# Expert outputs stored in 8 KB runs from half partitions, and three semaphores by turns for the Pool queue

## The chip, the cores and the metric

The kernel runs on one core of a Trainium2 chip. The metric is the device time of one execution in microseconds (us). Four runs before the change took 180.51 to 180.61 us, with a median of 180.54.

TensorE (PE) multiplies matrices, VectorE (DVE) and ScalarE (ACT) copy and apply functions, GpSimd (POOL) and SyncE (SP) issue transfers. Sixteen DMA engines carry out the transfers. A transfer is cut into packets, one for each contiguous run of bytes, and these are spread over the sixteen engines. Each issuing engine has its own queue, in which transfers start in the order in which they were issued.

## The reference

Eight experts, each with its own 256 tokens and two weight matrices; everything is float32 in memory:

```python
n_experts, capacity, hidden, expert_hidden = 8, 256, 512, 2048
# x [8, 256, 512], w1 [8, 512, 2048], w2 [8, 2048, 512]
h = np.matmul(x, w1)
h = np.maximum(h, 0)
return np.matmul(h, w2).astype(np.float32)
```

The weights are 64 MB, x and the output 4 MB each.

## The kernel before

**Transfers in.** x comes in two parts: SP loads a quarter as float32 (`x_head`, line 131), which VectorE casts to bfloat16 (line 132); Pool loads the rest and casts it on the way (line 146). All weights are loaded by Pool and cast to bfloat16 on the way (line 184), in the order of the list `loads` (lines 114 to 120): w1 and w2 of experts 0 and 1, then of 2 and 3, w1 of 4 and 5, w2 of 4, w2 of 5, w1 and w2 of 6, w1 of 7, and w2 of 7 in two halves. There are four places (`NS`) for the weights of an expert, so from expert 4 on a load waits until the expert four before it has used its weights (lines 166 to 170). w2 of experts 2 and 3 also waits for the transposes, since x lies in its place.

Every load adds 16 to a semaphore when it has landed. There is one such semaphore for each kind of weight and place, and one for the second half (`d_w`, `d_half`, lines 85 to 90). `landed[i]` is the semaphore and the count of load i. SP waits for the loads one after the other and passes each on to TensorE (lines 136 to 138).

**Computation.** TensorE transposes x (lines 290 to 318). VectorE and ScalarE copy the results from PSUM to `xT`, each one half of the tokens, four times (`copy_xt`, lines 193 to 197). In PSUM the columns stand by residue of the token number, and the copy puts them into the order that makes token `p * 2 + m` of an expert row `p` of output tile `m`.

Then the loop over experts (`expert`, line 397) has two halves of the hidden layer, 64 matmuls into `h_ps` with four ReLU activations on ScalarE, and 32 matmuls into `o_ps[0]` and `o_ps[1]`, one PSUM bank for 128 tokens each. VectorE copies each `o_ps[m]` to `out_sb[:, e, m, :]` (line 211); the last one is ScalarE's (line 231). TensorE takes `c_o` at the end of each half of the hidden layer (line 386), so that it doesn't write over outputs that are still to be copied.

**Transfers out.** Partition `p` of `out_sb` has tokens `2p` and `2p + 1` of each expert, 4 KB that are contiguous in the output. Experts 0 to 6 go out in one transfer by Pool, here called the gather (line 187), expert 7 in one by SP (line 140). Pool issues the gather when a small store of 1 KB (line 175) has landed. This store stands in the queue ahead of the second half of w2 of expert 7 and so tells when the loads before it are done. VectorE adds to `s_event` after experts 4 and 6 (line 214); the small store waits for the first of these, the gather for the second.

Of the kernel before, what the change touches and what calls it, by code (L numbers as in the profile page):

```python
# [8 lines left out]
FP32 = mybir.dt.float32  # L9
# [7 lines left out]
def kernel(  # L17
# [8 lines left out]
    P = 128  # L26
    E, C, H = x.shape
    F = w1.shape[2]
    MC = C // P
# [3 lines left out]
    R = E * C // P  # L33

    HEAD = 4

    NS = 4
# [8 lines left out]

    x_v = x.rearrange("e (pp r) k -> (e pp) (r k)", r=R)
    w1_v = w1.rearrange("e (p ko) n -> p e (ko n)", ko=K1)  # L50
    w2_v = w2.rearrange("e (p h j) n -> p e h (j n)", h=2, j=JH)
    out_v = out.rearrange("e (p mo) k -> p e (mo k)", mo=MC)


    places, free = {}, FIRST_FREE
# [1 line left out]
    def allot(name, shape, dtype):  # L57
        nonlocal free
        places[name] = free
        t = nc.alloc_sbuf_tensor_at(name, shape, dtype, offset=free)  # L60
        free += math.prod(shape[1:]) * mybir.dt.size(dtype)
        return t


    out_sb = allot("out_sb", [P, E, MC, H], FP32)
    w1_sb = allot("w1_sb", [P, NS, K1 * F], BF16)
    w2_sb = allot("w2_sb", [P, NS, K2 * H], BF16)
    xT = allot("xT", [P, K1, MC, E * P], BF16)
# [4 lines left out]
    x_sb = w2_sb[:, 2, :]  # L73
    X_AT = W2_AT + 2 * K2 * H * 2

    xt_ps = [nc.alloc_psum_tensor(f"xt_ps{i}", [P, R // MC, P], BF16) for i in range(MC)]
    h_ps = [nc.alloc_psum_tensor(f"h_ps{i}", [P, GJ * C], FP32) for i in range(UG)]
    o_ps = [nc.alloc_psum_tensor(f"o_ps{i}", [P, H], FP32) for i in range(MC)]

    def sem(name):  # L80
        return tc.alloc_semaphore(name)

    d_w = {
        (w, i): sem(f"d_w{w}_{i}")
        for w, slots in [(1, (0, 2, 3)), (2, (0, 1, 2, 3))]
        for i in slots
    }
    d_half, d_pool, d_last = sem("d_half"), sem("d_pool"), sem("d_last")  # L90


    s_event = sem("s_event")
    s_pe, v_last = sem("s_pe"), sem("v_last")

    def after_transposes(n):
        return s_pe, n

    def after_hidden(e, groups):
        return s_pe, K1 * MC + e * (NG + MC) + groups  # L100

    def after_outputs(e, halves):
        return s_pe, K1 * MC + e * (NG + MC) + NG + halves
# [10 lines left out]
    loads = []  # L114
# [3 lines left out]
    for e in range(6, E - 1):  # L118
        loads += [(1, (e,), 0, 2), (2, (e,), 0, 2)]
    loads += [(1, (E - 1,), 0, 2), (2, (E - 1,), 0, 1), (2, (E - 1,), 1, 1)]  # L120
    landed, counts = [], {}
    for w, es, h, _ in loads:
        s = d_half if h else d_w[w, es[0] % NS]
        counts[id(s)] = counts.get(id(s), 0) + 16
        landed.append((s, counts[id(s)]))

# [6 lines left out]
    with tc.tile_critical(no_gpsimd_drain=True):  # L133

        sp = nc.sync
        for i, (w, es, h, n) in enumerate(loads):
            sp.wait_ge(*landed[i])
            sp.sem_inc((c_w1, c_w2)[w - 1], n * len(es) if w == 2 else len(es))
        sp.wait_ge(v_last, MC)
        sp.dma_start(  # L140
            out_v[:, E - 1, :], out_sb[:, E - 1].rearrange("p m h -> p (m h)")
        ).then_inc(d_last, 16)


        pool = nc.gpsimd
        pool.dma_start(x_sb[:, HEAD * H:], x_v[:, HEAD * H:]).then_inc(d_pool, 16)  # L146
        pool.memset(identity[:], 0.0).then_inc(s_event)  # L147
        pool.wait_ge(s_event, 1)

# [1 line left out]
            out=identity[:],  # L151
# [7 lines left out]
        for i, (w, es, h, n) in enumerate(loads):  # L159


            old = es[-1] - NS
            if w == 2 and 2 in es:
                tc.wait_critical_data_deps()
                pool.wait_ge(*after_transposes(K1 * MC))
            if old >= 0 and h == 0:
                if w == 1:
                    pool.wait_ge(*after_hidden(old, NG))
                else:
                    pool.wait_ge(*after_outputs(old, MC))  # L170
            if i == len(loads) - 1:


                pool.wait_ge(s_event, 3)
                pool.dma_start(  # L175
                    out_v[:16, 0, :16], out_sb[:16, 0, 0, :16]
                ).then_inc(d_pool, 16)
            e, ne, at_slot = es[0], len(es), es[0] % NS
            if w == 2:
                src = w2_v[:, e:e + ne, h:h + n, :].rearrange("p e h n -> p e (h n)")  # L180
                dst = w2_sb[:, at_slot:at_slot + ne, h * JH * H:(h + n) * JH * H]
            else:
                src, dst = w1_v[:, e:e + ne, :], w1_sb[:, at_slot:at_slot + ne, :]
            pool.dma_start(dst, src).then_inc(landed[i][0], 16)  # L184
        pool.wait_ge(s_event, 4)
        pool.wait_ge(d_pool, 32)
        pool.dma_start(  # L187
            out_v[:, :E - 1, :], out_sb[:, :E - 1].rearrange("p e m h -> p e (m h)")
        ).then_inc(d_pool, 16)

        def copy_xt(copy, ko, m):
            return copy(  # L194
                xT[:, ko, m].rearrange("k (ep r2) -> k ep r2", r2=R // MC),
                xt_ps[m][:].rearrange("k r2 ep -> k ep r2"),
            )


        dve = nc.vector  # L200
        dve.sem_inc(c_xt[0], 1)
        for ko in range(K1):
            dve.wait_ge(*after_transposes(ko * MC + 1))
            copy_xt(dve.tensor_copy, ko, 0).then_inc(c_xt[0])
        dve.sem_inc(c_o, MC)
        for e in range(E):
            for m in range(MC):
                if e == E - 1 and m == 1:
                    break
                dve.wait_ge(*after_outputs(e, m + 1))  # L210
                cp = dve.tensor_copy(out_sb[:, e, m, :], o_ps[m][:])  # L211
                cp.then_inc(v_last if e == E - 1 else c_o)
            if e in (4, E - 2):
                dve.drain().then_inc(s_event)  # L214
# [16 lines left out]
        act.copy(out_sb[:, E - 1, 1, :], o_ps[1][:]).then_inc(v_last)  # L231

# [3 lines left out]
        pe = nc.tensor  # L236
# [45 lines left out]
        def last_column(step):  # L282

            return (P - 1) * step * 2
# [25 lines left out]
                t.then_inc(s_pe)  # L310

        pe.wait_ge(s_event, 2)
        pe.wait_ge(d_pool, 16)
# [119 lines left out]


        pool.drain()
        pool.wait_ge(d_pool, 48).then_inc(s_event)
        pool.wait_ge(d_last, 16).then_inc(s_event)


# [28 lines left out]
```

## Time and profile before

| what | value |
|---|---|
| median of four runs | 180.54 us |
| the profiled execution, its own time | 180.51 us |
| its span, first to last instruction | 178.7 us |
| TensorE busy | 126.9 us, 71% of the span |
| ScalarE, VectorE, Pool busy | 38.7, 15.8 and 10.2 us |
| bytes read from and written to memory | 71.30 MB and 4.20 MB |
| Pool's queue, share of the 16 DMA engines' span | 97.3% |
| SP's queue | 2.4% |
| gather of experts 0 to 6 (3,584 KB), issue to landing | 12.9 us |
| store of expert 7 (512 KB), issue to landing | 4.7 us |
| x by SP (1,024 KB) and by Pool (1,536 KB after the cast) | 4.7 and 11.5 us |
| copy of one output tile, VectorE, 128 x 512 | 686 ns |
| copy of one part of xT, 128 x 1024: VectorE, ScalarE | 1,224 and 1,012 ns |

A packet's bytes are counted as written, so a load that casts float32 to bfloat16 reads twice as many as are shown. Windows are stretches of the span with the busy time of each engine, the DMA share (mean busy share of the 16 DMA engines; it can pass 1 a little, since a packet is counted where it starts) and the bytes moved in GB/s. "Us to landing" runs from the start of the issuing instruction until the semaphore has its full count, and so has the time in the queue in it. Beside these views the trace has a record of every DMA packet (start, duration, bytes, queue) and of every semaphore update at a landing.

### The profile page before, as it was taken

The page shows a single profiled execution, that of the slowest core. Times are in us where ns is not written, and L with a number is a line of the kernel's source. Part 1 is how long each engine was busy: PE and PEld are TensorE (multiplying, and loading weights), DVE is VectorE, ACT ScalarE, POOL GpSimd, SP SyncE. Part 2 cuts the span into 40 slices and gives each one's busy share as a digit, 9 for nine tenths or more (in the row PEclk, how much of TensorE's full clock was granted, in tenths as well). Part 3 has the DMA queues.
Part 4 walks back from the last instruction along what each step waited for, and adds up shares of the span by engine and source line. Part 5 has one row for each costly group of instructions (what it writes and reads, how often), then busy time and mean ns, then how long its engine had stood idle before and what let it go on. Part 6 is the DMA issues. An engine that isn't in the chain of part 4 may idle for free. (4 is left out here: it accounts for less than half of the span.)

```text
span 178.7 us, 2096 instructions
## 1 busy us (share of the span) xinstructions
PE 126.9 (71%) x832; PEld 89.4 (50%) x832; DVE 15.8 (9%) x20; ACT 38.7 (22%) x38; POOL 10.2 (6%) x21
## 2 busy tenths in 40 slices
PE   0008610793049999991079999999999999969950
PEld 0006600693014794791024884794695596369420
DVE  0204320000000200200000200200200200110010
ACT  0202420044000152062000251152063044015210
POOL 6100010000000002101000101100020000002000
PEclk9999999999559999999558999999999999999998
DMA  6999998998998999999899899999999989989996
GB/s 211 244 216 209 235 224 187 235 231 187 227 235 191 220 235 209 202 235 227 183 235 235 183 227 235 194 216 235 213 198 235 227 183 235 235 180 220 328 423 258
DMA packets 3744, 40.37 MB, mean 226 GB/s; under 512 B 288, under 2 KB 288, under 8 KB 1312
## 3 DMA queue, kind: packets, MB, share of 16 engines
q0 software_dynamic: 3456, 38.80, 97.3%
q1 hardware_dynamic: 288, 1.57, 2.4%
HBM read 71.30 MB, written 4.20 MB: 422 GB/s over the span
## 5 line engine op out<-in xcount | busy, mean ns | idle before, releaser
L264 PE MATMUL o_ps<-w_sb,hT 128*128 x256 | 60.3, 396 | 18.8 <-PEq L239 18.8
L264 PE MATMUL h_ps<-xT,w_sb 128*128 x512 | 60.6, 280 | 11.2 <-PEq L239 11.2
L264 PEld LDWEIGHTS h_ps<-xT,w_sb 128*128 x512 | 57.6, 146 | 15.1 <-issue 11.9
L225 ACT ACTIVATE hT<-h_ps 128x1024 bf16<-128x1024 f32 x32 | 32.7, 1023 | 109.6 <-PE h_ps L264 109.6
L264 PEld LDWEIGHTS o_ps<-w_sb,hT 128*128 128x128 bf16 x256 | 25.3, 101 | 51.2 <-issue 24.4
L211 DVE COPY out_sb<-o_ps 128x512 f32<-128x512 f32 x15 | 9.7, 686 | 139.7 <-PE o_ps L264 139.7
L264 PE MATMUL xt_ps<-identity,w_sb 128*128 128x128 bf16 x64 | 7.6, 312 | 15.5 <-PEq L239 15.5
L264 PEld LDWEIGHTS xt_ps<-identity,w_sb 128*128 x64 | 6.5, 147 | 16.3 <-issue 16.3
L184 POOL DMA_DIRECT2D w_sb<-in_w_dram x12 | 7.4, 618 | 105.2 <-PE h_ps L264 56.5
L194 ACT COPY xT<-xt_ps 128x1024 bf16<-128x1024 bf16 x4 | 4.0, 1012 | 11.8 <-PE xt_ps L264 11.8
L194 DVE COPY xT<-xt_ps 128x1024 bf16<-128x1024 bf16 x4 | 4.9, 1224 | 11.8 <-PE xt_ps L264 11.8
L187 POOL DMA_DIRECT2D out_dram<-out_sb x1 | 1.0, 962 | 33.1 <-DMA out_dram<-out_sb 33.1
L194 ACT ACT_TABLE_LOAD x1 | 1.3, 1283 | 7.0 <-DVE w_sb L132 7.0
L231 ACT COPY out_sb<-o_ps 128x512 f32<-128x512 f32 x1 | 0.6, 585 | 5.9 <-PE o_ps L264 5.9
L132 DVE CAST w_sb<-x_head 128x2048 bf16<-128x2048 f32 x1 | 1.2, 1227 | 5.5 <-DMA x_head<-in_x_dram 5.5
L175 POOL DMA_DIRECT2D out_dram<-out_sb x1 | 0.5, 509 | 14.7 <-DVEq L214 14.7
L146 POOL DMA_DIRECT2D w_sb<-in_x_dram x1 | 0.7, 679 | 0.8 <-POOLq L452 0.8
L150 POOL TENSOR_SCALAR_AFFINE_SELECT identity<-identity 128x128 bf16<-128x128 bf16 x1 | 0.3, 282 | 0.2 <-POOL identity L147 0.2
L147 POOL MEMSET identity<- 128x128 bf16 x1 | 0.2, 223 | 0.0
L452 POOL MEMSET const-float32-0.0<- 128x1 f32 x1 | 0.1, 92 | 0.2 <-issue 0.2
L452 POOL MEMSET const-bfloat16-1.0<- 128x1 bf16 x1 | 0.1, 95 | 0.0
L452 POOL MEMSET const-uint8-127<- 128x1 uint8 x1 | 0.1, 95 | 0.0
(1 smaller groups left out, 0.1 us busy)
## 6 DMA issues: line engine op xcount, KB each, us to landing
w_sb<-in_w_dram POOLq DMA_DIRECT2D x5, 4096.0 KB, 47.9
w_sb<-in_w_dram POOLq DMA_DIRECT2D x5, 2048.0 KB, 51.0
out_dram<-out_sb POOLq DMA_DIRECT2D x1, 3584.0 KB, 12.9
w_sb<-in_w_dram POOLq DMA_DIRECT2D x2, 1024.0 KB, 43.2
w_sb<-in_x_dram POOLq DMA_DIRECT2D x1, 1536.0 KB, 11.5
x_head<-in_x_dram SPq DMA_DIRECT2D x1, 1024.0 KB, 4.7
out_dram<-out_sb SPq DMA_DIRECT2D x1, 512.0 KB, 4.7
out_dram<-out_sb POOLq DMA_DIRECT2D x1, 1.0 KB, 33.6
```

What stands on the lines that cost most here:

```text
L132: nc.vector.tensor_copy(x_sb[:, :HEAD * H], x_head[:])
L146: pool.dma_start(x_sb[:, HEAD * H:], x_v[:, HEAD * H:]).then_inc(d_pool, 16)
L150: pool.affine_select(out=identity[:], in_=identity[:], compare_op=mybir.AluOpType.not_equal, fill=1.0, base=0, pattern=[[-1, P]], channel_ ...
L175: pool.dma_start(out_v[:16, 0, :16], out_sb[:16, 0, 0, :16]).then_inc(d_pool, 16)
L184: pool.dma_start(dst, src).then_inc(landed[i][0], 16)
L187: pool.dma_start(out_v[:, :E - 1, :], out_sb[:, :E - 1].rearrange("p e m h -> p e (m h)")).then_inc(d_pool, 16)
L194: return copy(xT[:, ko, m].rearrange("k (ep r2) -> k ep r2", r2=R // MC), xt_ps[m][:].rearrange("k r2 ep -> k ep r2"),)
L211: cp = dve.tensor_copy(out_sb[:, e, m, :], o_ps[m][:])
L225: act.activation(hT[:, g * GJ:(g + 1) * GJ, :].rearrange("p a c -> p (a c)"), h_ps[g % UG][:], mybir.ActivationFunctionType.Relu,).then_in ...
L231: act.copy(out_sb[:, E - 1, 1, :], o_ps[1][:]).then_inc(v_last)
L264: return pe.add_instruction(inst)
L452: nc = _bacc.Bacc("TRN2", target_bir_lowering=False, num_devices=1)
```

## The change

It has two parts.

1. *Semaphores.* The nine semaphores for Pool's transfers in and out (`d_w`, `d_half`, `d_pool`) become three, used by turns; `d_last` for SP's store stays. A transfer with number i uses semaphore i mod 3, and before it is issued Pool waits until transfer i - 3 has landed. The numbers are: 0 the part of x, 1 to 11 the loads but the last, 12 the small store, 13 the last load, 14 the gather, 15 a further store.

2. *Outputs.* Experts 0 to 5 are kept in pairs: the even one of a pair on partitions 0 to 63, the odd one on 64 to 127. A partition has four tokens of its expert, `4q` to `4q + 3`, which are 8 KB and contiguous in the output. Since a PSUM tile still has 128 tokens on 128 partitions, VectorE copies it in two halves of 64 partitions. For token `4q + 2t + m` to come out on row `t * 64 + q` of tile `m`, the columns of `xT` for these experts get another order, and each copy to `xT` becomes three (two for experts 0 to 5, one for 6 and 7). The gather has experts 0 to 5. Expert 6 goes out in a transfer of its own right behind it on Pool's queue, in runs of 4 KB as before, and expert 7 by SP as before. VectorE adds to `s_event` after experts 0, 5 and 6 instead of 4 and 6; the small store waits for the first, the gather for the second, expert 6's store for the third.

```diff
+    HP = P // 2
+    PAIRS = E // 2 - 1
+    out_pairs = out[:2 * PAIRS].rearrange("(i s) (q r) k -> s q i (r k)", s=2, r=2 * MC)
+    out_v = out.rearrange("e (p m) k -> p e (m k)", m=MC)
...
-    out_sb = allot("out_sb", [P, E, MC, H], FP32)
+    out_sb = allot("out_sb", [P, PAIRS, 2 * MC, H], FP32)
+    last_sb = allot("last_sb", [P, 2, MC, H], FP32)
...
-    d_half, d_pool, d_last = sem("d_half"), sem("d_pool"), sem("d_last")
+    d_pool, d_last = [sem(f"d_pool{i}") for i in range(3)], sem("d_last")
...
+    of_load = [i + 1 for i in range(len(loads) - 1)] + [len(loads) + 1]
+    small, bulk, bulk2 = len(loads), len(loads) + 2, len(loads) + 3
+
+    def landed(i):
+        return d_pool[i % 3], 16 * (i // 3 + 1)
...
+        def queue(i, dst, src):
+            if i >= 3:
+                pool.wait_ge(*landed(i - 3))
+            pool.dma_start(dst, src).then_inc(d_pool[i % 3], 16)
...
-            pool.dma_start(dst, src).then_inc(landed[i][0], 16)
+            queue(of_load[i], dst, src)
+        pool.wait_ge(*landed(small))
         pool.wait_ge(s_event, 4)
-        pool.wait_ge(d_pool, 32)
-        pool.dma_start(
-            out_v[:, :E - 1, :], out_sb[:, :E - 1].rearrange("p e m h -> p e (m h)")
-        ).then_inc(d_pool, 16)
+        queue(bulk, out_pairs, out_sb[:].rearrange("p i r h -> p i (r h)"))
+        pool.wait_ge(s_event, 5)
+        queue(bulk2, out_v[:, E - 2, :], last_sb[:, 0].rearrange("p m h -> p (m h)"))
...
         def copy_xt(copy, ko, m):
+            EP = 2 * PAIRS
+            for t in range(2):
+                copy(
+                    xT[:, ko, m, :EP * P].rearrange(
+                        "k (e t pp r4) -> k t e pp r4", e=EP, t=2, r4=R // 4
+                    )[:, t],
+                    xt_ps[m][:, :, :EP * (P // E)].rearrange(
+                        "k (r4 t) (e pp) -> k t e pp r4", t=2, e=EP
+                    )[:, t],
+                )
             return copy(
-                xT[:, ko, m].rearrange("k (ep r2) -> k ep r2", r2=R // MC),
-                xt_ps[m][:].rearrange("k r2 ep -> k ep r2"),
+                xT[:, ko, m, EP * P:].rearrange("k (ep r2) -> k ep r2", r2=R // MC),
+                xt_ps[m][:, :, EP * (P // E):].rearrange("k r2 ep -> k ep r2"),
             )
+
+        def copy_out(copy, e, m):
+            if e >= 2 * PAIRS:
+                return copy(last_sb[:, e - 2 * PAIRS, m, :], o_ps[m][:])
+            i, s = divmod(e, 2)
+            for t in range(2):
+                inst = copy(
+                    out_sb[s * HP:(s + 1) * HP, i, t * MC + m, :],
+                    o_ps[m][t * HP:(t + 1) * HP, :],
+                )
+            return inst
...
-            if e in (4, E - 2):
+            if e in (0, E - 3, E - 2):
                 dve.drain().then_inc(s_event)
...
-        pool.wait_ge(d_pool, 48).then_inc(s_event)
+        for i in (bulk, bulk2):
+            pool.wait_ge(*landed(i)).then_inc(s_event)
         pool.wait_ge(d_last, 16).then_inc(s_event)
```

More of the change, by code (lines that the diff above doesn't have):

```diff
@@ L51 @@
     w2_v = w2.rearrange("e (p h j) n -> p e h (j n)", h=2, j=JH)
-    out_v = out.rearrange("e (p mo) k -> p e (mo k)", mo=MC)
+    HP = P // 2
+    PAIRS = E // 2 - 1
+    out_pairs = out[:2 * PAIRS].rearrange("(i s) (q r) k -> s q i (r k)", s=2, r=2 * MC)
+    out_v = out.rearrange("e (p m) k -> p e (m k)", m=MC)
     places, free = {}, FIRST_FREE
@@ L81, in sem @@
         return tc.alloc_semaphore(name)
[L85 to L89, printed above, removed]
-    d_half, d_pool, d_last = sem("d_half"), sem("d_pool"), sem("d_last")
+    d_pool, d_last = [sem(f"d_pool{i}") for i in range(3)], sem("d_last")
     s_event = sem("s_event")
@@ L120 @@
     loads += [(1, (E - 1,), 0, 2), (2, (E - 1,), 0, 1), (2, (E - 1,), 1, 1)]
[L121 to L125, printed above, removed]
+    of_load = [i + 1 for i in range(len(loads) - 1)] + [len(loads) + 1]
+    small, bulk, bulk2 = len(loads), len(loads) + 2, len(loads) + 3
+    def landed(i):
+        return d_pool[i % 3], 16 * (i // 3 + 1)
     x_pool = ctx.enter_context(tc.tile_pool(name="x_pool", bufs=1))
@@ L136 @@
         for i, (w, es, h, n) in enumerate(loads):
-            sp.wait_ge(*landed[i])
+            sp.wait_ge(*landed(of_load[i]))
             sp.sem_inc((c_w1, c_w2)[w - 1], n * len(es) if w == 2 else len(es))
@@ L140 @@
         sp.dma_start(
-            out_v[:, E - 1, :], out_sb[:, E - 1].rearrange("p m h -> p (m h)")
+            out_v[:, E - 1, :], last_sb[:, 1].rearrange("p m h -> p (m h)")
         ).then_inc(d_last, 16)
         pool = nc.gpsimd
-        pool.dma_start(x_sb[:, HEAD * H:], x_v[:, HEAD * H:]).then_inc(d_pool, 16)
+        def queue(i, dst, src):
+            if i >= 3:
+                pool.wait_ge(*landed(i - 3))
+            pool.dma_start(dst, src).then_inc(d_pool[i % 3], 16)
+        queue(0, x_sb[:, HEAD * H:], x_v[:, HEAD * H:])
         pool.memset(identity[:], 0.0).then_inc(s_event)
@@ L174 @@
                 pool.wait_ge(s_event, 3)
-                pool.dma_start(
-                    out_v[:16, 0, :16], out_sb[:16, 0, 0, :16]
-                ).then_inc(d_pool, 16)
+                queue(small, out_pairs[0, :16, 0, :16], out_sb[:16, 0, 0, :16])
             e, ne, at_slot = es[0], len(es), es[0] % NS
@@ L183 @@
                 src, dst = w1_v[:, e:e + ne, :], w1_sb[:, at_slot:at_slot + ne, :]
-            pool.dma_start(dst, src).then_inc(landed[i][0], 16)
+            queue(of_load[i], dst, src)
+        pool.wait_ge(*landed(small))
         pool.wait_ge(s_event, 4)
-        pool.wait_ge(d_pool, 32)
-        pool.dma_start(
-            out_v[:, :E - 1, :], out_sb[:, :E - 1].rearrange("p e m h -> p e (m h)")
-        ).then_inc(d_pool, 16)
+        queue(bulk, out_pairs, out_sb[:].rearrange("p i r h -> p i (r h)"))
+        pool.wait_ge(s_event, 5)
+        queue(bulk2, out_v[:, E - 2, :], last_sb[:, 0].rearrange("p m h -> p (m h)"))
         def copy_xt(copy, ko, m):
+            EP = 2 * PAIRS
[8 more added lines that the diff above has]
+                )
             return copy(
-                xT[:, ko, m].rearrange("k (ep r2) -> k ep r2", r2=R // MC),
-                xt_ps[m][:].rearrange("k r2 ep -> k ep r2"),
-            )
+                xT[:, ko, m, EP * P:].rearrange("k (ep r2) -> k ep r2", r2=R // MC),
+                xt_ps[m][:, :, EP * (P // E):].rearrange("k r2 ep -> k ep r2"),
+            )
+        def copy_out(copy, e, m):
[8 more added lines that the diff above has]
+            return inst
         dve = nc.vector
@@ L210 @@
                 dve.wait_ge(*after_outputs(e, m + 1))
-                cp = dve.tensor_copy(out_sb[:, e, m, :], o_ps[m][:])
+                cp = copy_out(dve.tensor_copy, e, m)
                 cp.then_inc(v_last if e == E - 1 else c_o)
-            if e in (4, E - 2):
+            if e in (0, E - 3, E - 2):
                 dve.drain().then_inc(s_event)
@@ L230 @@
         act.wait_ge(*after_outputs(E - 1, MC))
-        act.copy(out_sb[:, E - 1, 1, :], o_ps[1][:]).then_inc(v_last)
+        copy_out(act.copy, E - 1, 1).then_inc(v_last)
         pe = nc.tensor
@@ L312 @@
         pe.wait_ge(s_event, 2)
-        pe.wait_ge(d_pool, 16)
+        pe.wait_ge(*landed(0))
         x_first = X_AT + last_column(K1)
```

## The prediction

> **What bounds the kernel now.** I read the page's slices first: the row of DMA shares shows whether the transfer engines ever rest.
>
> ```profile
> DMA  6999998998998999999899899999999989989996
> GB/s 211 244 216 209 235 224 187 235 231 187 227 235 191 220 235 209 202 235 227 183 235 235 183 227 235 194 216 235 213 198 235 227 183 235 235 180 220 328 423 258
> q0 software_dynamic: 3456, 38.80, 97.3%
> ```
>
> They rest only at both ends. A slice is 4.47 us and a packet of weights takes over 1 us, so the GB/s row beats; longer windows are steadier. Columns: busy times by engine, then PE clock, DMA share, GB/s written.
>
> ```profile
> 24.00:30.00 6.00, 0.00 (x0) 0.00 (x0) 0.00 (x0) 0.10 (x1) 0.07 (x1) 1.00 1.02 218
> 48.00:54.00 6.00, 2.40 (x6) 0.87 (x7) 0.00 (x0) 0.00 (x0) 0.00 (x0) 0.50 1.03 218
> 84.00:90.00 6.00, 0.00 (x0) 0.00 (x0) 0.00 (x0) 0.00 (x0) 0.00 (x0) 0.59 1.03 218
> 108.00:114.00 6.00, 6.00 (x31) 2.85 (x30) 0.27 (x1) 0.01 (x1) 0.00 (x0) 1.00 1.01 216
> 166.00:167.00 1.00, 1.00 (x6) 0.42 (x5) 0.00 (x0) 0.46 (x1) 0.00 (x0) 1.00 0.82 176
> 167.00:168.00 1.00, 1.00 (x6) 0.49 (x5) 0.00 (x0) 0.00 (x0) 0.00 (x0) 1.00 0.96 385
> 171.00:172.00 1.00, 1.00 (x7) 0.39 (x4) 0.00 (x0) 0.00 (x0) 0.00 (x0) 1.00 1.02 422
> 176.00:177.00 1.00, 0.00 (x0) 0.00 (x0) 0.00 (x0) 0.00 (x0) 0.00 (x0) 1.00 0.98 401
> 177.00:178.00 1.00, 0.00 (x0) 0.00 (x0) 0.00 (x0) 0.00 (x0) 0.00 (x0) 0.62 0.07 25
> ```
>
> Loads are cast, so 218 GB/s written is 436 GB/s read. A boundary between two loads lies inside 48 to 54 us (TensorE waits for w2 of experts 0 and 1 until 51.6) and doesn't show. At 167 us the stores take over at 422 GB/s and run to 177.3. In 84 to 90 TensorE is idle while the transfers run.
>
> The chain of waits names TensorE, but only up to the issue of the last store:
>
> ```profile
> 158.04 0.04 issue
> 158.09 7.32 PE h_ps L264 x64
> 165.40 6.97 PE o_ps L264 x32
> 172.37 0.02 issue
> 172.39 0.58 ACT out_sb L231
> ```
>
> Who decides after that? The last store is issued at 173.00, and the trace's packet records have its first packet on a DMA engine at 175.60, just as that engine ends the gather (all move in step, the last 0.47 us behind the first). At the start the same queue's x load, issued at 0.74, had a packet moving at 1.75. So the store could have run from 174.0 and stood 1.6 us behind the gather. The DMA engines are the bound from 1.75 to 177.3; a change matters if it opens a hole there, changes what a packet costs, or changes the ends.
>
> **The issue order.** The timeline of the Pool queue shows when each of the last transfers is issued:
>
> ```profile
> 107.25 0.53 POOL L184 DMA_DIRECT2D w_sb<-in_w_dram  x1 [6.59 <-PE h_ps L264]
> 114.20 0.53 POOL L184 DMA_DIRECT2D w_sb<-in_w_dram  x1 [6.43 <-PE o_ps L264]
> 129.43 0.51 POOL L175 DMA_DIRECT2D out_dram<-out_sb  x1 [14.69 <-DVEq L214]
> 129.93 0.55 POOL L184 DMA_DIRECT2D w_sb<-in_w_dram  x1
> 163.58 0.96 POOL L187 DMA_DIRECT2D out_dram<-out_sb  x1 [33.09 <-DMA out_dram<-out_sb]
> ```
>
> All weights are queued by 130.5, the last of them over 30 us before it moves. The trace's landing records (us): x 12.7; w1 of experts 0 and 1 at 32.1, w2 51.4; w1 of 2 and 3 at 70.8, w2 90.1; w1 of 4 and 5 at 109.5, w2 of 4 at 119.2, of 5 at 128.9; expert 6 138.5 and 148.2; w1 of 7 at 157.9, first half of its w2 162.8, the small store 163.0, second half 167.7, gather 176.5, last store 177.7.
>
> **Part 1, three semaphores by turns.** Transfer i is now issued only when i-3 has landed. Taking the wake as 0.59 us (the small store's landing at 162.99 to the gather's issue at 163.58), the loads go out at about 13.3 (w1 of 2 and 3), 32.7, 67.4 (still the wait for expert 1's hidden layer), then 71.4, 90.7, 110.1, 119.8, 129.5, 139.1, small store 148.8, second half of w2 158.5. Each time the queue still holds i-2 and i-1. In the middle that is at least two 2,048 KB loads, 19.4 us. It is least for the second half of w2: only the first half and the small store lie ahead, which the first DMA engine finishes at 162.03. The gather bounds the time from issue to first packet: 163.58 to 166.89, so at most 3.31 us. 157.91 + 0.59 + 3.31 = 161.8 is still 0.2 us before 162.03; the x load behind the SP load gives a like bound, 1.23 to 4.61. I take **0**; lower bound 0, upper bound below as a rival. Behind the waiting instruction on Pool stand only later transfers, each slowed as counted. The gather's own trigger, the small store, is in its old place in the queue, so the gather is issued at 163.6 as before, behind 4 us of load. SP's counts go by the same landings.
>
> **Part 2, the gather.** Before: 7 x 128 packets of 4 KB, 56 for each DMA engine. After: 3 x 128 of 8 KB and 128 of 4 KB, so 24 and 8. The packet records give the period on one DMA engine: 155.3 ns for 4 KB in the gather (65,536 B in 155.3 ns is the 422 GB/s above), 306.0 ns for 8 KB in the SP queue's uncast x load between 3.7 and 4.3 us. That is another direction of transfer, but it is the nearest row: 24 x (310.6 - 306.0) = **-0.11 us**. Bounds: 0, if 8 KB costs just two packets of 4 KB; -0.24, if the store reaches the loads' 436 GB/s (27.25 per DMA engine, 8 KB in 300.6 ns: 24 x 10.0). A loss is excluded as far as rows go: every steady row with larger packets is as fast or faster. One more transfer means one more completion packet per DMA engine: 6 ns from such a packet to the next in the store stage, **+0.01**; at most 0.06, which is 1% of a 6 us window with a boundary in it.
>
> The Trainium skill, "DMA: Bandwidth & Descriptors", section on the anatomy of a DMA from GpSimd, puts a fixed cost of about 2.0 us on each such transfer. By that the split into two stores would add 2.0 and give 182.4. The window 48 to 54 speaks against it in a full queue.
>
> The same page (why a DMA increments its semaphore by 16) says that a transfer is spread over the engines by its outermost dimension, and the new view of the output has an outermost dimension of 2. If that were kept, 2 of 16 engines would carry the gather. The two outer steps can join into one of 128 equal steps (64 rows of 8 KB are one expert's 512 KB, and the next expert begins there), so I expect 16; no row here shows a gather of that form.
>
> **Part 3, the copies.** Twelve output copies become 24 of half the partitions. From the groups: 686 ns each; if a half costs as much (bounds 343 and 686), an expert's copies take 2.7 us instead of 1.3. They hide under the next expert's hidden layer (7.28 us), whose two takes come 3.6 and 7.3 us on. The xT copies become three pieces each: the fixed part of a DVE copy is about 0.15 us (1,224 ns for 1,024 columns, 686 for 512), ScalarE's 0.16, so 2 x 0.15 x 4 rounds = 1.2 us more, at most 9.8 if each piece cost a whole copy. The transposes end at 24.1 and TensorE stands until 32.25 for w1: 8.1 us of cover. Even past it TensorE waits 9.7 us more for w2 at 51.6, and x lands long before. Were that cover gone, the first expert would start 1.2 us late; the stream of transfers, which sets the end, would not. The two plain experts' copies don't change, so the last store is still issued at 173.0, with 1.5 us to spare. **0**.
>
> **Part 4, the end.** After 177.7 come the closing barriers and one instruction that clears 26 semaphores in 179 ns; six fewer, at the 5 ns between two clears, **-0.03** (bounds 0 and -0.04).
>
> **Sum:** -0.11 + 0.01 - 0.03 = -0.13 us on the profiled execution (180.51, span 178.7 and 1.8 around it), which stands 0.03 under the median; taken off the median: 180.54 - 0.13 = **180.41**. Its own range is 180.26 (-0.24, -0.04, 0) to 180.60 (0, 0, +0.06).
>
> **Rivals.** (a) *The 8 KB runs bring nothing*: 180.52. For it: 4 KB packets already leave only 3% between 422 and 436. (b) *The store reaches the load's rate*: 180.26; for it the 436, against it the measured 306 ns. (c) *A late second half*, on the slow side: the second half of w2 reaches the queue after 162.03, all engines stop, and everything behind moves by the gap, since stores follow loads. It decides when landing-to-first-packet passes 4.1 us. If the issue took as long as the last store from issue to landing (4.7 us), the gap is 157.91 + 0.59 + 4.7 - 162.03 = 1.2 us: 181.6. Against it: the 3.31 bound. (d) *The gather goes through two engines*, because its view starts with a step over two experts: 192 packets of 306 ns each, 58.8 us instead of 7.3: about 232. (e) *The change does not do what it says*: should the gather be cut to 4 KB packets again, it is (a).
>
> **Chances.** Forecast with (a) and (b), which differ by less than a measurement of this kernel can tell from no change (0.2%, 0.36 us): 0.80, of it 0.62 for the forecast itself, 0.12 for (a) with (e), 0.06 for (b). (c) and smaller holes of its kind 0.11, (d) 0.02. Faster by over 0.36 has no row behind it, as the bounds end at -0.28: 0.07 for what I don't see. So faster 0.07, same 0.80, slower 0.13. The range leaves 2 in 10 out: 180.2 to 180.75, the low end just past (b), the high end a hole of 0.2 us.
>
> **What would show it.** Windows at 168 to 174 at 427 to 428 GB/s instead of 422 for (forecast), 422 for (a), 436 for (b), and near 53 for (d). For Part 1: Pool's last load issue at 158.5, and the windows from 160 to 164 without a DMA share under 0.9; a hole there is (c). The last store landing at 177.6, and TensorE's last expert starting at 158.1 as before. I am wrong if w1 of expert 7 lands later than 158.0, or if the last store's issue moves past 174.5.

## The result, and the profile after

The changed kernel takes 180.86 us in the median (39 runs, 180.62 to 181.31) against 180.54 before (59 runs). The ratio is 1.0017, with a 95% interval of 1.0012 to 1.0022: slower by 0.32 us, where -0.13 was forecast and 180.75 was the upper end of the range. The profiled execution took 180.99 us, with a span of 179.0.

First the windows of the changed kernel that answer to those of before (last columns: DMA share, GB/s):

```profile
48.00:54.00 6.00, 2.31 (x6) 0.90 (x7) 0.00 (x0) 0.00 (x0) 0.00 (x0) 0.50 1.03 218
84.00:90.00 6.00, 0.00 (x0) 0.00 (x0) 0.00 (x0) 0.00 (x0) 0.00 (x0) 0.66 1.03 218
108.00:114.00 6.00, 6.00 (x30) 2.70 (x29) 0.00 (x0) 0.48 (x1) 0.53 (x1) 1.00 1.01 216
166.00:167.00 1.00, 1.00 (x6) 0.49 (x5) 0.00 (x0) 0.55 (x1) 0.00 (x0) 1.00 0.80 164
167.00:168.00 1.00, 1.00 (x7) 0.43 (x5) 0.00 (x0) 0.00 (x0) 0.00 (x0) 1.00 1.02 410
171.00:172.00 1.00, 1.00 (x6) 0.47 (x5) 0.00 (x0) 0.00 (x0) 0.00 (x0) 1.00 1.04 442
176.00:177.00 1.00, 0.00 (x0) 0.00 (x0) 0.00 (x0) 0.00 (x0) 0.00 (x0) 0.50 0.88 360
177.00:178.00 1.00, 0.00 (x0) 0.00 (x0) 0.00 (x0) 0.00 (x0) 0.00 (x0) 0.50 0.07 29
```

The stream of loads is as it was: 218 GB/s, no hole where a transfer was issued late. At the end the share falls earlier than before (0.88 at 176 to 177, against 0.98): some DMA engines are done, others are not. The timeline of Pool's queue:

```profile
110.10 0.53 POOL L155 DMA_DIRECT2D w_sb<-in_w_dram  x1 [18.79 <-DMA w_sb<-in_w_dram]
119.78 0.53 POOL L155 DMA_DIRECT2D w_sb<-in_w_dram  x1 [9.15 <-PE h_ps L295]
129.52 0.53 POOL L155 DMA_DIRECT2D w_sb<-in_w_dram  x1 [9.20 <-DMA w_sb<-in_w_dram]
139.16 0.53 POOL L155 DMA_DIRECT2D w_sb<-in_w_dram  x1 [9.11 <-DMA w_sb<-in_w_dram]
148.91 0.51 POOL L155 DMA_DIRECT2D out_dram<-out_sb  x1 [9.23 <-DMA w_sb<-in_w_dram]
158.29 0.55 POOL L155 DMA_DIRECT2D w_sb<-in_w_dram  x1 [8.87 <-DMA w_sb<-in_w_dram]
163.53 0.77 POOL L155 DMA_DIRECT2D out_dram<-out_sb  x1 [4.69 <-DMA out_dram<-out_sb]
164.30 0.57 POOL L155 DMA_DIRECT2D out_dram<-last_sb  x1
```

Each of the first six waits for a landing and comes within 0.25 us of the time worked out in the prediction. (The row of 119.78 names TensorE, whose part was long done: the kernel before issued this load at 100.13. What came just ahead of it is the landing of w2 of expert 4, at 119.26.) The chain of waits has only moved by 0.08 us:

```profile
158.17 7.32 PE h_ps L295 x64
165.49 6.97 PE o_ps L295 x32
172.46 0.02 issue
172.48 0.59 ACT last_sb L221
```

Where are the 0.32 us, then? The trace's records of packets and landings cut one execution of each kernel into pieces (us):

| piece | before | after | difference |
|---|---|---|---|
| landing of w1 of expert 7 | 157.91 | 158.00 | +0.09 |
| from there to the end of the last load's last packet | 9.46 | 9.78 | +0.32 |
| from there to the end of the last store's last packet | 9.95 | 9.84 | -0.11 |
| from there to the end of the span | 1.42 | 1.37 | -0.05 |
| measured time less span | 1.77 | 2.00 | +0.23 |

The pieces add up to 0.48, the difference of these two executions (180.99 and 180.51); the medians differ by 0.32. The first row varies from execution to execution (157.75 to 158.09 in the kernels here, e6_half_copies apart), so its 0.09 is no part of the change. Two rows were not in the sum. *The tail of the last load*: each DMA engine has eight packets of the second half of w2, which took 625 ns each before. After the change 14 of 128 took 650 to 890, all of them the seventh or eighth of their engine, between 165.7 and 167.8 us; the engine that was last but one lost most, 0.40 us, and so ended last. *The time outside the span*: over the 41 recorded runs of the changed kernel it is 1.99 us in the mean; in the runs of the kernel before, 1.76 to 1.77.

### The profile page after: what moved, and what is told of

The parts are those of the page before. It is cut to its first block, busy times and chain, and to the rows that moved or that the text cites. A ratio compares the mean times of both kernels' runs of the same rounds, so it can differ in the third digit from the quotient of the medians.

```text
span 179.0 us, 2137 instructions
## 1 busy us (share of the span) xinstructions
PE 128.0 (72%) x832; PEld 90.0 (50%) x832; DVE 25.2 (14%) x40; ACT 39.2 (22%) x46; POOL 10.6 (6%) x22
## 5 line engine op out<-in xcount | busy, mean ns | idle before, releaser
L295 PE MATMUL o_ps<-w_sb,hT 128*128 x256 | 61.1, 400 | 18.1 <-PEq L270 18.1
L256 ACT ACTIVATE hT<-h_ps 128x1024 bf16<-128x1024 f32 x32 | 32.8, 1024 | 109.1 <-PE h_ps L295 109.1
L224 DVE COPY out_sb<-o_ps 64x512 f32<-64x512 f32 x24 | 16.5, 689 | 104.6 <-PE o_ps L295 104.2
L206 ACT COPY xT<-xt_ps 128x384 bf16<-128x384 bf16 x8 | 3.4, 482 | 11.8 <-PE xt_ps L295 11.8
L206 DVE COPY xT<-xt_ps 128x384 bf16<-128x384 bf16 x8 | 4.1, 552 | 11.8 <-PE xt_ps L295 11.8
L221 DVE COPY last_sb<-o_ps 128x512 f32<-128x512 f32 x3 | 2.0, 689 | 25.8 <-PE o_ps L295 25.8
L221 ACT COPY last_sb<-o_ps 128x512 f32<-128x512 f32 x1 | 0.6, 586 | 5.9 <-PE o_ps L295 5.9
L214 DVE COPY xT<-xt_ps 128x256 bf16<-128x256 bf16 x4 | 1.7, 415 | 0.0
L214 ACT COPY xT<-xt_ps 128x256 bf16<-128x256 bf16 x4 | 1.6, 390 | 0.0
L155 POOL DMA_DIRECT2D out_dram<-last_sb x1 | 0.6, 574 | 0.0
```

Of the source, the lines that this page charges most:

```text
L155: pool.dma_start(dst, src).then_inc(d_pool[i % 3], 16)
L206: copy(xT[:, ko, m, :EP * P].rearrange("k (e t pp r4) -> k t e pp r4", e=EP, t=2, r4=R // 4)[:, t], xt_ps[m][:, :, :EP * (P // E)].rearran ...
L214: return copy(xT[:, ko, m, EP * P:].rearrange("k (ep r2) -> k ep r2", r2=R // MC), xt_ps[m][:, :, EP * (P // E):].rearrange("k r2 ep -> k ...
L221: return copy(last_sb[:, e - 2 * PAIRS, m, :], o_ps[m][:])
L224: inst = copy(out_sb[s * HP:(s + 1) * HP, i, t * MC + m, :], o_ps[m][t * HP:(t + 1) * HP, :],)
L256: act.activation(hT[:, g * GJ:(g + 1) * GJ, :].rearrange("p a c -> p (a c)"), h_ps[g % UG][:], mybir.ActivationFunctionType.Relu,).then_in ...
```

## The experiments

Each kernel was timed beside the kernel before on the same chip. "Outside" is measured time less span. "Tail" is worked out: difference of the span's median from that of the kernel before, less what the stores bring (-0.11 with 8 KB packets, +0.01 for two gathers) and less -0.03 where three semaphores take the place of nine. The intervals of the ratios are some 0.1% each way (0.18 us), so one tail alone says little under 0.2; the groups say more. The code cuts below show the lines that matter. They stand against the kernel before or the changed kernel, as the text names them, and else against an earlier run: e8_early against e2_outputs, e12_act_pieces against e5_xt_pieces, e14_six_first and e17_small_old against e11_relu_order, e15_half_contig against e7_half_4k, e16_plain_stride against e9_dest, e18_small_new against e13_8k_plain.

| run | before, us | this, us | ratio, 95% interval | outside | tail |
|---|---|---|---|---|---|
| changed kernel | 180.54 | 180.86 | 1.0017 (1.0012 to 1.0022) | 1.99 | 0.23 |
| e1_turns | 180.60 | 180.58 | 0.9995 (0.9979 to 1.0011) | 1.79 | -0.01 |
| e2_outputs | 180.60 | 181.05 | 1.0023 (1.0012 to 1.0033) | 2.01 | 0.32 |
| e3_six_by_sp | 180.60 | 180.93 | 1.0019 (1.0008 to 1.0029) | 2.01 | 0.22 |
| e4_split | 180.60 | 180.58 | 0.9995 (0.9986 to 1.0003) | 1.78 | -0.03 |
| e5_xt_pieces (one run) | 180.48 | 180.72 | | 1.92 | |
| e6_half_copies (one run) | 180.48 | 181.43 | | 1.76 | |
| e7_half_4k | 180.48 | 181.05 | 1.0038 (1.0021 to 1.0055) | 2.00 | 0.35 |
| e8_early | 180.48 | 181.17 | 1.0031 (1.0020 to 1.0043) | 2.01 | 0.55 |
| e9_dest | 180.55 | 180.59 | 1.0001 (0.9992 to 1.0010) | 1.77 | 0.03 |
| e10_plain_dest | 180.55 | 180.75 | 1.0008 (0.9999 to 1.0017) | 2.00 | 0.00 |
| e11_relu_order | 180.55 | 180.71 | 1.0004 (0.9995 to 1.0013) | 1.77 | 0.29 |
| e12_act_pieces (one run) | 180.55 | 180.70 | | 1.93 | |
| e13_8k_plain | 180.61 | 180.50 | 0.9996 (0.9985 to 1.0007) | 1.76 | 0.00 |
| e14_six_first | 180.61 | 180.67 | 1.0004 (0.9994 to 1.0013) | 1.77 | 0.19 |
| e15_half_contig | 180.61 | 180.96 | 1.0019 (1.0010 to 1.0028) | 2.00 | 0.14 |
| e16_plain_stride | 180.61 | 180.63 | 0.9997 (0.9986 to 1.0009) | 1.77 | 0.01 |
| e17_small_old | 180.52 | 180.61 | 1.0007 (0.9998 to 1.0016) | 1.78 | 0.22 |
| e18_small_new | 180.52 | 180.51 | 1.0002 (0.9993 to 1.0011) | 1.78 | 0.09 |

### The change in its parts

The kernel before with the turns alone, and the changed kernel with the old semaphores:

```diff
-            pool.dma_start(dst, src).then_inc(landed[i][0], 16)
+            queue(of_load[i], dst, src)
```

> The kernel before with the three semaphores by turns, outputs as before. Theories: A, the last load, now issued late (158.3 us instead of 129.9), has its last packets slowed; B, the second output transfer that Pool issues while the last load moves slows it; C, the gather in 8 KB packets from the half-partition layout slows it. A: 180.95 (180.54 + 0.45 of stall - 0.03), packets of 8,192 B with cast over 640 ns near 166 us, landings of the last load spread over 0.9 us. B and C: 180.51, all such packets at 625 ns, spread 0.5 us.

```diff
-        def queue(i, dst, src):
-            if i >= 3:
-                pool.wait_ge(*landed(i - 3))
-            pool.dma_start(dst, src).then_inc(d_pool[i % 3], 16)
+        def queue(s, dst, src):
+            pool.dma_start(dst, src).then_inc(s, 16)
```

> The changed kernel with the nine semaphores of before, so all loads are queued early; outputs as changed. A: 180.43 (180.54 - 0.11), spread of the last load's landings 0.5 us. B and C: 180.85 to 180.9, spread 0.9 us.

Expert 6 by SP instead of Pool, and the old gather split in two:

```diff
+        sp.wait_ge(s_event, 5)
+        sp.dma_start(
+            out_v[:, E - 2, :], last_sb[:, 0].rearrange("p m h -> p (m h)")
+        ).then_inc(d_last, 16)
```

> The changed kernel with expert 6's outputs issued by SP after the last load has landed, so that Pool issues the gather alone while the last load moves. B: 180.43, spread of the last load's landings 0.5 us. A and C: 180.85, spread 0.9 us.

```diff
-            out_v[:, :E - 1, :], out_sb[:, :E - 1].rearrange("p e m h -> p e (m h)")
+            out_v[:, :E - 2, :], out_sb[:, :E - 2].rearrange("p e m h -> p e (m h)")
         ).then_inc(d_pool, 16)
+        pool.wait_ge(s_event, 5)
+        pool.dma_start(
+            out_v[:, E - 2, :], out_sb[:, E - 2].rearrange("p m h -> p (m h)")
+        ).then_inc(d_pool, 16)
```

> The kernel before with its gather of 4 KB runs split into experts 0 to 5 and expert 6, semaphores and layout as before. B: 181.0 (180.54 + 0.45 of stall), spread of the last load's landings 0.9 us. A and C: 180.55, spread 0.5 us.

The turns alone and a second transfer alone cost nothing beyond the intervals (180.58 each, where A and B had 180.95 and 181.0), and e3_six_by_sp, without the second transfer on Pool's queue, keeps the loss: A and B fall. All of the loss that shows is in the outputs. It is in two pieces, since both kernels with the new outputs have 2.01 us outside the span and those with the old ones 1.78 or 1.79. This first showed that the loss is not in the span alone, which the expectations had not reckoned with.

### What lies outside the span

```diff
+            n = R // MC
+            for lo, hi in [(0, 48), (48, 96), (96, 128)]:
+                inst = copy(
+                    xT[:, ko, m, lo * n:hi * n].rearrange("k (ep r2) -> k ep r2", r2=n),
+                    xt_ps[m][:, :, lo:hi].rearrange("k r2 ep -> k ep r2"),
+                )
+            return inst
```

> The kernel before with each copy to xT cut into three pieces (by columns, order as before), so VectorE and ScalarE have 8 instructions more each. The measured time less the span was 1.77 us in the kernels with the old outputs and 2.0 in those with the new ones. D, that this comes from VectorE's added output copies: 1.77 here. E, that it comes from the added xT copies: 2.0. F, that it comes from the form of the new transfers: 1.77.

```diff
+                parts = [(0, P)] if e >= 6 else [(0, P // 2), (P // 2, P)]
+                for lo, hi in parts:
+                    cp = dve.tensor_copy(out_sb[lo:hi, e, m, :], o_ps[m][lo:hi, :])
```

> The kernel before with the output copies of experts 0 to 5 cut into two halves of the partitions (layout as before), so VectorE has 12 instructions more. Time less span: D 2.0 us, E and F 1.77.

```diff
-            for lo, hi in [(0, 48), (48, 96), (96, 128)]:
+            for lo, hi in [(0, 48), (48, 96), (96, 128)] if m else [(0, 128)]:
```

> The kernel before with the xT copies in three pieces on ScalarE alone (8 instructions more), VectorE's whole. Time less span: 1.92 us as with pieces on both engines, if ScalarE's program is the cause; 1.77, if VectorE's is.

Pieces on both engines give 1.92, pieces on ScalarE alone 1.93, halves on VectorE alone 1.76. So D falls, and E has most of the 2.0 that it gave, but not all. These are single runs; in the profiled executions of the kernels with the old copies the same difference is 1.76 to 1.78. (In e6_half_copies' single run well over a hundred packets of the loads between 20 and 111 us were slow, as in no other profile; its time says nothing of the halves.) The groups of e12_act_pieces show that only ScalarE's copies differ there:

```profile
L196 ACT COPY xT<-xt_ps 128x384 bf16<-128x384 bf16 (+1 forms) x12 | 4.5, 452 | 11.4 <-PE xt_ps L267 11.4
L196 DVE COPY xT<-xt_ps 128x1024 bf16<-128x1024 bf16 x4 | 4.9, 1224 | 11.8 <-PE xt_ps L267 11.8
```

Eight more instructions on ScalarE, all executed by 25 us, so lengthen what lies outside the span by 0.15. For the remaining 0.08 of the changed kernel the copies of x in the form that it uses, the added output copies, or both are needed; this was not taken apart. The next kernel takes all of it away. It makes the token order where hT is written, so the xT copies are whole, and copies both tiles of an expert in one instruction for each half of the partitions:

```diff
+                if e < 2 * PAIRS:
+                    to = to.rearrange("p a (m t q) -> p (a m) t q", m=MC, t=2)
+                    fr = fr.rearrange("p (am q t) -> p am t q", q=HP, t=2)
...
+                    cp = dve.tensor_copy(
+                        out_sb[s * HP:(s + 1) * HP, i, t * MC:(t + 1) * MC, :].rearrange("p m h -> p (m h)"),
+                        o_all[t * HP:(t + 1) * HP, :],
+                    )
+                cp.then_inc(c_o, MC)
```

> The changed kernel with the token order made by the ReLU's write of hT instead of the copies to xT (these are whole again), and with one copy of 64 x 1,024 for both tiles in place of two of 64 x 512, so that ScalarE and VectorE have as many instructions as before. If the time outside the span comes from the added xT pieces: 1.77 us outside, otherwise 2.0. With the 8 KB runs the last load's tail stays slow by J: span 178.9, time 180.65. By K, if the copies are the cause: 180.4 to 180.65.

```profile
L251 ACT ACTIVATE hT<-h_ps 128x1024 bf16<-128x1024 f32 x32 | 32.7, 1023 | 109.6 <-PE h_ps L290 109.6
L221 DVE COPY out_sb<-o_all 64x1024 f32<-64x1024 f32 x12 | 14.7, 1222 | 106.3 <-PE o_all L290 106.2
L205 ACT COPY xT<-xt_ps 128x1024 bf16<-128x1024 bf16 x4 | 4.0, 1012 | 11.8 <-PE xt_ps L290 11.8
```

These are its groups. The ReLU with a reordered read takes 1,023 ns as before, so the order is free there, and the outside is 1.77 again. It has the new transfers, so F falls as well. With that, e11_relu_order stands 0.16 us above the kernel before, the changed kernel 0.32; its tail is still slow.

### The tail of the last load

Is it the packet size, the layout (which partition holds which tokens), or the moment of the issue?

```diff
+        for h in range(2):
+            queue(
+                bulk + h,
+                out_pairs[:, :, :, h * MC * H:(h + 1) * MC * H],
+                out_sb[:, :, h * MC:(h + 1) * MC].rearrange("p i r h -> p i (r h)"),
+            )
```

> The changed kernel with the gather of experts 0 to 5 as two transfers of 4 KB runs each, from the same half-partition layout. G, that packets of 8 KB make the last load's tail slow: from the landing of the first half of the last weights to that of the second 4.9 to 5.1 us as with the old outputs, span 178.75 median. H, that the layout does, whatever the size: 5.2 to 5.4 us, span 179.1. Time 180.75 by G, 181.1 by H (both with 2.0 us outside the span).

```diff
-                pool.wait_ge(s_event, 3)
-                queue(d_pool, out_pairs[0, :16, 0, :16], out_sb[:16, 0, 0, :16])
...
-        pool.wait_ge(d_pool, 32)
```

> The changed outputs with the nine semaphores of before, but no small store and no wait for it: the gather is issued as soon as the outputs of expert 5 are copied (near 145 us), expert 6's store near 158. I, that the issue of an output transfer slows what is moving some 2 us later: slow packets near 147 and 160 us, none at 165 to 167; the time as large as with the changed kernel. G and H: slow packets at 165 to 167 as before, 180.9 to 181.05.

Pool's timeline of e8_early shows that the last stores are now issued long before they move:

```profile
113.36 1.05 POOL L158 DMA_DIRECT2D w_sb<-in_w_dram  x2 [6.42 <-PE o_ps L292]
144.20 0.76 POOL L158 DMA_DIRECT2D out_dram<-out_sb  x1 [29.78 <-DVEq L242]
156.90 0.57 POOL L158 DMA_DIRECT2D out_dram<-last_sb  x1 [11.94 <-DVEq L242]
```

No packet near 147 or 160 us was slow; 37 of the last load's 128 were, from 164.5 us on. So I falls: the slow packets belong to the place in the queue, just ahead of the stores, and not to the issue. e7_half_4k has the slow tail with 4 KB packets (5.38 us between the two landings), which spoke for the layout. Then one factor at a time, destination and layout:

```diff
+        pairs = out[:E - 2].rearrange("(i s) (q r) k -> s q i (r k)", s=2, r=2 * MC)
+        for h in range(2):
+            pool.dma_start(
+                pairs[:, :, :, h * MC * H:(h + 1) * MC * H],
+                out_sb[:, 3 * h:3 * (h + 1)].rearrange("p e m h -> p e (m h)"),
+            ).then_inc(d_pool, 16)
```

> The kernel before, whose plain layout in on-chip memory goes out as two transfers of 4 KB runs to the places of the 8 KB runs: partition p writes at p x 8 KB and not at p x 4 KB, so the rows of experts 0 to 5 lie in another order in the output. J, that the step of 8 KB between the partitions' places in memory slows the last load's tail: 5.2 to 5.4 us from the landing of the first half of the last weights to that of the second, span 179.1, time 180.85 to 180.9. K, that the half-partition copies or the layout on chip do: 4.9 to 5.1 us, span 178.8, time 180.6.

```diff
+            out_v[:, :2 * PAIRS, :],
+            out_sb[:].rearrange("p i (s r) h -> p (i s) (r h)", s=2),
```

> The changed kernel whose gather goes in 4 KB runs to the places of the old gather (p x 4 KB, one transfer); half-partition copies and layout on chip as changed, so the rows of experts 0 to 5 lie in another order in the output. J: 4.9 to 5.1 us between the two landings, span 178.75, time 180.75 (2.0 outside the span). K: 5.2 to 5.4 us, span 179.05, time 181.05.

e9_dest came out as K gave it (5.02 us between the two landings, 180.59), e10_plain_dest as J did (5.10 us, 180.75). So neither ingredient alone: J and K fall both. (In e10_plain_dest the small store went back to rows 4 KB apart as well; more of that below.) Packet size, source step and order of the stores next:

```diff
+        pool.dma_start(
+            pairs, out_sb[:, :E - 2].rearrange("p (i s) m h -> p i (s m h)", s=2)
+        ).then_inc(d_pool, 16)
```

> The kernel before, plain layout and copies, whose gather of experts 0 to 5 goes in 8 KB packets (two experts that lie side by side on chip) to the places of the changed gather, and expert 6 behind it; the rows of experts 0 to 5 lie in another order in the output. If the packet size slows the last load's tail: span 178.95 median, time 180.72. If the half-partition copies are needed for it: span 178.68, time 180.45 (the gather's gain alone).

```diff
+        pool.wait_ge(s_event, 5)
+        queue(bulk, out_v[:, E - 2, :], last_sb[:, 0].rearrange("p m h -> p (m h)"))
+        queue(bulk2, out_pairs, out_sb[:].rearrange("p i r h -> p i (r h)"))
```

> The kernel with the token order made by the ReLU's write, with expert 6's 4 KB store issued ahead of the 8 KB gather. If only the packets right behind the last load matter, the tail is as with the old outputs: span 178.62, time 180.40, under the kernel before. If it is anything else about the gather: 180.7 as with the gather first.

```diff
-                out_sb[:, :, h * MC:(h + 1) * MC].rearrange("p i r h -> p i (r h)"),
+                out_sb[:].rearrange("p i (s r) h -> p (i s) (r h)", s=2)[:, 3 * h:3 * (h + 1)],
```

> The changed kernel with two transfers of 4 KB packets to the 8 KB places, each of which reads three 4 KB rows that lie side by side on chip (the rows of experts 0 to 5 lie in another order in the output). If the step of 8 KB between source rows was the cause where two such transfers were slow: span 178.78, time 180.78. If the half-partition copies together with the 8 KB places are: span 179.05, time 181.05.

```diff
-                out_sb[:, 3 * h:3 * (h + 1)].rearrange("p e m h -> p e (m h)"),
+                out_sb[:, h:E - 2:2].rearrange("p e m h -> p e (m h)"),
```

> The kernel before, plain layout and copies, with two transfers of 4 KB packets to the 8 KB places, each of which reads rows 8 KB apart on chip (the rows of experts 0 to 5 lie in another order in the output). If the source step is the cause: span 179.05, time 180.82. If not: span 178.8, time 180.58.

The size of the packets alone is not the cause: e13_8k_plain has the same gather and the same stores of experts 6 and 7 as e2_outputs, from the same addresses on chip to the same places, and a tail of 0.00 against 0.32. Its windows from 164 to 170 us:

```profile
164.00:166.00 2.00, 2.00 (x20) 2.00 (x19) 0.00 (x0) 1.28 (x2) 0.93 (x2) 1.00 1.13 233
166.00:168.00 2.00, 1.95 (x14) 1.31 (x14) 0.00 (x0) 1.28 (x2) 0.00 (x0) 1.00 0.90 287
168.00:170.00 2.00, 2.00 (x11) 0.89 (x10) 0.00 (x0) 0.01 (x1) 0.00 (x0) 1.00 1.01 430
```

And the same windows of e2_outputs:

```profile
164.00:166.00 2.00, 1.95 (x16) 1.51 (x15) 0.00 (x0) 1.28 (x2) 0.53 (x1) 1.00 1.14 217
166.00:168.00 2.00, 2.00 (x11) 0.88 (x9) 0.00 (x0) 0.39 (x1) 0.00 (x0) 1.00 0.85 242
168.00:170.00 2.00, 2.00 (x11) 0.92 (x10) 0.00 (x0) 0.00 (x0) 0.00 (x0) 1.00 1.05 446
```

In this one execution of each, less is moved in e2_outputs around the passage from loads to stores (217 and 242 GB/s against 233 and 287). By the packet records the last load's packets took 4.59 us longer there than 625 ns each, 0.29 us for each of the 16 engines; in e13_8k_plain 0.60, or 0.04 for each. The steady 430 GB/s of e13_8k_plain is the gain of 8 KB packets, against 420 to 422 before. The source step isn't the cause either (e16_plain_stride), and a 4 KB store ahead of the gather doesn't heal it (e14_six_first). e15_half_contig, at 180.96, is nearer to what the half-partition copies with the 8 KB places would give (181.05) than to 180.78, but its interval reaches both. One difference was left between the two groups, the small store's place:

```diff
-                queue(small, out_pairs[0, :16, 0, :16], out_sb[:16, 0, 0, :16])
+                queue(small, out_v[:16, 0, :16], out_sb[:16, 0, 0, :16])
```

> The kernel with the token order made by the ReLU's write, its small store alone put back to rows 4 KB apart (the gather writes over them later). M, that the place of the small store decides how the last load's tail goes: span 178.65 median, time 180.42, under the kernel before by 0.1 to 0.2. N, that it does not and the half-partition outputs do in another way: span 178.9, time 180.7.

```diff
-                    out_v[:16, 0, :16], out_sb[:16, 0, 0, :16]
+                    rows[0, :16, 0, :16], out_sb[:16, 0, 0, :16]
```

> The plain layout with 8 KB packets, its small store alone moved to rows 8 KB apart; as in that run, the rows of experts 0 to 5 lie in another order in the output. M: span 178.95, time 180.72. N: span 178.7, time 180.5.

180.51 and 180.61 speak for N: moving the small store neither brings the slow tail (0.09) nor takes it away (0.22). e8_early, which has no small store and the largest tail of all (0.55), says the same. **What is shown** is a pattern in the medians: the nine kernels, the changed one among them, that have both the half-partition outputs and the 8 KB places have tails of 0.14 to 0.55, and the seven with one or neither -0.03 to 0.09.

Two things make this weaker than it looks. That the half-partition outputs without the 8 KB places do no harm rests on e10_plain_dest alone. And the packet records, of one execution for each kernel, don't part the two groups: of the last load's 128 packets, 12 to 37 took over 630 ns in the nine (0.05 to 0.55 us more for a DMA engine on the average), 6 to 17 in the seven (0.02 to 0.14, the most in e10_plain_dest), and none in the kernel before and the three that kept its transfers and semaphores (e5, e6 and e12). So some packets were slow wherever semaphores or stores were changed, and how much of it reaches the time differs from run to run: the eleven runs of e17_small_old go from 180.37, below all 21 of the kernel before beside it, to 180.99.

**Why** the two ingredients together lose most stays open. e2_outputs and e13_8k_plain also differ in the small store's place, in the moment at which the last load is issued (115.5 and 129.2 us; the changed kernel and e1_turns, with a tail and without one, both issue it at 158.3), and in copies that VectorE and ScalarE finish 20 us before the tail. No row in the traces joins any of these to a packet of the last load. Whether the place of the tensors in memory, which may differ from kernel to kernel, plays a part wasn't tried.

No kernel of these beats the one before beyond the interval. The best forms of the change (ReLU order, whole copies) are at 1.0004 to 1.0007 (e11_relu_order, e14_six_first, e17_small_old).

## Why the prediction was wrong

**The bound** was right: the DMA engines set the end, and TensorE's chain had 1.4 us to spare (last store issued at 173.09, so it could have run from 174.1, as the x load ran 1.0 after its issue; its first packet came at 175.53). In e1_turns's profiled execution the last store was issued only at 174.64, and the stores still took the 9.95 us of before. Neither of the prediction's signs of being wrong came: w1 of expert 7 landed at 158.00 and the last store was issued at 173.09. They watched for a late load or a late TensorE, and the loss came behind both; what missed was the last store's landing, 177.97 for 177.6.

**Part 1** was right: issue times (but for the one at 67.4, which came at 67.90 without effect), no hole, and 0 us within e1_turns's interval. Rival (c) did not come. The tightest point, the second half of w2, was issued at 158.29 and moved without a gap.

**Part 2** was right in what it counted, the gather. From the last load's end to the last store's end the packet records give 9.95 or 9.96 us in every kernel with 4 KB packets, and 9.84 in every one with 8 KB packets: -0.11 as worked out. The 306 ns, taken from a load, hold for the store (306 there too), and the stores from 168 to 174 us went at 429 GB/s, where 427 to 428 was the sign of the forecast and 422 the rate before. A second transfer cost 0.00 (e4_split), so the 2.0 us of the Trainium skill, "DMA: Bandwidth & Descriptors", section on the anatomy of a DMA, are not paid in a full queue. All sixteen engines carried the gather, and rival (d) did not come. The step that failed is "a loss is excluded as far as rows go": it looked at the store's own packets. The loss fell on the load ahead of them, which the sum put at nothing: +0.23 us in the median, for which the trace of before had no sign: all 128 packets of its last load took 624 or 625 ns.

**Part 3** had the copies' durations right, and its cover held. These are the groups of the changed kernel:

```profile
L224 DVE COPY out_sb<-o_ps 64x512 f32<-64x512 f32 x24 | 16.5, 689 | 104.6 <-PE o_ps L295 104.2
L206 ACT COPY xT<-xt_ps 128x384 bf16<-128x384 bf16 x8 | 3.4, 482 | 11.8 <-PE xt_ps L295 11.8
L206 DVE COPY xT<-xt_ps 128x384 bf16<-128x384 bf16 x8 | 4.1, 552 | 11.8 <-PE xt_ps L295 11.8
L214 ACT COPY xT<-xt_ps 128x256 bf16<-128x256 bf16 x4 | 1.6, 390 | 0.0
```

A half copy takes 689 ns, what a whole one took, and the transposes end 0.6 us later than before, where 1.2 was worked out. But "**0**" for them failed in another place, together with the sum's "1.8 around it", which it took for a constant: the added copies made this 2.0, +0.23 us. Of that, 0.15 is shown to come with eight more instructions on ScalarE (e12_act_pieces); which of the other copies bring the remaining 0.08 wasn't taken apart.

**Part 4** was right: -0.05 from the last packet to the span's end, also in e1_turns, where -0.03 was worked out and -0.04 was the bound.

So -0.11 - 0.03 + 0.23 + 0.23 = +0.32, the measured difference. This closes by its making, since the tail's 0.23 is what the other three leave of the medians. The forecast's sum was right inside its own terms, and two terms were missing from it. The range, to 180.75, had room for a hole of 0.2 us and not for these two.

## What to carry to other kernels

Where a change is worth tenths of a microsecond, compare measured time less span as well as the span: instructions added where they delay nothing (here on ScalarE, in the shadow of a load) can still lengthen the part that no view of the profile shows. See whether a permutation can be moved into an instruction that runs anyway; here the ReLU's read took it at no cost. When the DMA engines set the end, look at what a new transfer does to the packets ahead of it, and time each ingredient alone and together, because here neither alone showed a loss in the median. One profiled execution is not enough for effects of this size.

## What the runs showed of the hardware

- Eight more ScalarE copies lengthened the time outside the span from 1.77 to 1.93 us (e12_act_pieces, one run); twelve more VectorE copies did not (1.76, e6_half_copies, one run).
- Three transfers in flight kept sixteen DMA engines as full as loads that were all queued early: 218 GB/s written with the cast.
- Stores went at 422 GB/s in 4 KB packets and 429 to 430 in 8 KB packets (168 to 174 us of the kernel before, the changed kernel and e13_8k_plain), 155.3 and 306 ns for each on one engine.
- At the passage from loads to stores, packets of the last load took up to 1,250 ns instead of 625 (6 to 37 of 128 over 630 ns where semaphores or stores were changed, none in the kernel before), the first of them before a store's first packet.
- A copy of half the partitions takes as long as one of all (689 and 686 ns), and one of 64 x 1,024 over two PSUM banks 1,222 ns.
